# Four row tiles of A loaded ahead of B's second k-tile, a shorter warm-up, and an earlier bias in a matmul, bias and tanh kernel

## The chip, the cores and the metric

The kernel runs on one core of a Trainium2 chip. The metric is the device time of the whole program in microseconds (us). The profile's span covers the same execution without its first and last steps, and is some 2 us shorter. Engines: TensorE (PE), VectorE (DVE), ScalarE (ACT), GpSimd (POOL), which here issues nearly all loads, and SyncE (SP).

## The reference

```
a: 4096 x 4096, b: 4096 x 4096, bias: 4096, all float32
out = tanh(a @ b + bias)
```

## The kernel before

A and B are loaded as float32, cast to float16 on the way, and multiplied as 8192 matmuls of 128 x 128 by 128 x 512. The change concerns the first 100 us, where the rows of A come in two groups of four 128-row tiles and only a part of K is there yet. "Part one" uses eight k-tiles. Group 0's row tiles are transposed on PE itself (with an identity), into a PSUM bank, copied out half by DVE and half by ACT; group 1's are transposed by DVE.

```python
    WARM = 16
    ...
    for i in range(WARM):                       # warm-up matmuls on zeros
        nc.tensor.matmul(warm, zeros[:, :P], zeros, start=i == 0, stop=i == WARM - 1)
    load_b_low(nc.sync, raw_b, 0, 0, 1)         # B's first k-tile, as float32
    nc.scalar.copy(b_cur[0][:, 0, :], raw_b[:, 0, :])
    ...
    def turn_nat(m):
        tp = psum.tile([P, KS, P], fp16, name="tp", tag="ps")
        for t in range(KS):
            nc.tensor.transpose(tp[:, t, :], nat[m][:, :, t], ident)
        h = KS // 2
        nc.vector.tensor_copy(ats[m][:, ds(0, h), :], tp[:, ds(0, h), :])
        nc.scalar.copy(ats[m][:, ds(h, h), :], tp[:, ds(h, h), :])
    ...
    load_nat(0)
    load_nat(1)
    ...
    load_b_next()
    for m in (2, 3):
        load_nat(m)
        load_b_next()
    while b_done[0] < KS:
        load_b_next()
    want_a("g1a", 2, 4 * P, 2 * Q, 0, KS)       # group 1's first A
    ...
    turn_nat(0)
    turn_nat(1)
    row(0, 0, 1)
    row(1, 0, 1)
    across(ps, (0, 1), 1, 1, 0)
    turn_nat(2)
    row(2, 0, 2)
    across(ps, (0, 1, 2), 2, 1, 0)
    turn_nat(3)
    row(3, 0, 3)
    across(ps, range(G), 3, KS - 2 - 3, 0)
    ...
    for m in range(G):
        turn1(m, ("g1a", "g1b"), 0, KS)         # DVE transposes for group 1
    down(ps, KS - 2, KS, put_aside)
    group1(0, KS, put_aside, before1)
```

`row(m, t0, nt)` multiplies one row tile by k-tiles t0 and following (two matmuls each), `across` goes over several row tiles per k-tile, `down` ends one PSUM bank after another.

Of the kernel before, what the change touches and what calls it, by code (L numbers as in the profile page):

```python
# [23 lines left out]
def kernel(  # L24
# [7 lines left out]
    nc = tc.nc  # L32
# [8 lines left out]
    J = NCW // NB  # L41
    TB = 4
    G = 4
    KS = 8
    AN = 3
    KM = 16
    WARM = 16

    singles = ctx.enter_context(tc.tile_pool(name="singles", bufs=1))
    bpool = ctx.enter_context(tc.tile_pool(name="bpool", bufs=2))  # L50
# [14 lines left out]
    def load_b_low(queue, dst, n0, t0, nt):  # L65

        src = b[ds(0, P * KS), ds(n0, NCW)].rearrange("(x t) n -> x t n", t=KS)
        queue.dma_start(out=dst, in_=src[:, ds(t0, nt), :])  # L68
# [32 lines left out]
    def load_bias(bias_bc, n0, queue):  # L101
        src = bias[ds(n0, NCW)]
        queue.dma_start(
            out=bias_bc,
            in_=bass.AP(tensor=src.tensor, offset=src.offset, ap=[[0, P], *src.ap]),
        )
# [12 lines left out]
    def want_a(key, uses, *where):  # L119
        queue.append((key, uses, lambda: load_a(*where)))  # L120

    def want(load):
        queue.append((None, 0, load))

    def turn(at, key, mb0, t0, nt):
        pump()
        transpose_a(at, staged[key][0], mb0, t0, nt)
        staged[key][1] -= 1
        if not staged[key][1]:
            live[0] -= 1  # L130
            pump()

    def mm(ps, at, bt, t, j, start, stop):
        nc.tensor.matmul(  # L134
            ps, at[:, t, :], bt[t // TB][:, t % TB, ts(j, NB)], start=start, stop=stop
        )
# [27 lines left out]
    def aside(m, j):  # L164
        return spill[(m * J + j) // 4][:, (m * J + j) % 4, :]
# [9 lines left out]
    def add_bias(m, j):  # L175
        nc.vector.tensor_tensor(  # L176
            out=aside(m, j), in0=aside(m, j), in1=bias_bc[:, ts(j, NB)], op=mybir.AluOpType.add
        )
# [4 lines left out]
    def banks():  # L183
        return [[psum.tile([P, NB], fp32, name="ps") for j in range(J)] for m in range(G)]

    def load_b_all(t0, nt):
        for q in (0, 2, 1, 3):
            load_b(b_cur, 0, t0, nt, q)

    def across(ps, ms, t0, nt, first):  # L190
        for t in range(t0, t0 + nt):
            for m in ms:
                for j in range(J):
                    mm(ps[m][j], ats[m], b_cur, t, j, t == first, False)
# [22 lines left out]
    warm = psum.tile([P, NB], fp32, name="ps")  # L217
    for i in range(WARM):
        nc.tensor.matmul(warm, zeros[:, :P], zeros, start=i == 0, stop=i == WARM - 1)  # L219

# [9 lines left out]
    def load_nat(m):  # L230
        nc.gpsimd.dma_start(  # L231
            out=nat[m], in_=a[ds(m * P, P), ds(0, P * KS)].rearrange("m (x t) -> m x t", t=KS)
        )

    def load_b_next():
        t = b_done[0]
        b_done[0] += 1
        load_b_low(nc.gpsimd, b_cur[t // TB][:, ds(t % TB, 1), :], 0, t, 1)
# [8 lines that stand above are left out]
# [5 lines left out]
        out=ident, in_=ident, compare_op=mybir.AluOpType.is_equal, fill=0.0,  # L252
        base=0, pattern=[[-1, P]], channel_multiplier=1,
    )
    load_b_next()
    for m in (2, 3):
        load_nat(m)
        load_b_next()
    while b_done[0] < KS:
        load_b_next()  # L260
    want_a("g1a", 2, 4 * P, 2 * Q, 0, KS)
# [4 lines left out]
    want_a("g1c", 2, 4 * P, 2 * Q, KS, KM - KS)  # L266
    want_a("g1d", 2, 6 * P, 2 * Q, KS, KM - KS)
    bias_bc = biasp.tile([P, NCW], fp32, name="bias_bc")
    SA = [(KM, 8), (KM + 8, 8)]
    for t, nt in SA:  # L270
        want_a(("g0", t), G, 0, G * Q, t, nt)
        for u in range(t, t + nt, TB):
            want(lambda u=u: load_b_all(u, TB))
    want(lambda: load_bias(bias_bc, 0, nc.gpsimd))
    for m in range(G):
        want_a(("g1", m), 1, (G + m) * P, Q, KM, KT - KM)
    todo = [(c, mi) for c in range(NC) for mi in range(MT) if (c, mi) >= (0, 2 * G)]
# [1 line left out]
    ps = []  # L279

    def row(m, t0, nt):
        if len(ps) == m:
            ps.append([psum.tile([P, NB], fp32, name="ps") for j in range(J)])
        across(ps, (m,), t0, nt, 0)

    turn_nat(0)
    turn_nat(1)
    row(0, 0, 1)
    row(1, 0, 1)
    across(ps, (0, 1), 1, 1, 0)  # L290
    turn_nat(2)
    row(2, 0, 2)
    across(ps, (0, 1, 2), 2, 1, 0)
    turn_nat(3)
    row(3, 0, 3)
    across(ps, range(G), 3, KS - 2 - 3, 0)

    def turn1(m, keys, t, nt):
        turn(ats[G + m], keys[m // 2], (m % 2) * Q, t, nt)
# [1 line left out]
    def turn0(m, t, nt):  # L301
        turn(ats[m], ("g0", t), m * Q, t, nt)
# [14 lines left out]
    ps = banks()  # L317
# [5 lines left out]
    def before2(m, j):  # L323
        if m >= 2 * G - 2:
            turn0(2 * (m - 6) + j, *SA[0])

# [3 lines left out]
    ps = banks()  # L330
    for i, (t, nt) in enumerate(SA):
        for m in range(G):
            if i:
                turn0(m, t, nt)
        across(ps, range(G), t, min(t + nt, KT - TB) - t, KM)

    def turn2(m):
        turn(ats[G + m], ("g1", m), 0, KM, KT - KM)

    for m in range(2 * G):  # L340
        for j in range(J):
            add_bias(m, j)
    turn2(0)
    down(ps, KT - TB, KT, end)

# [26 lines left out]
    for i, (c, mi) in enumerate(todo):  # L372
        if mi == 0:
            b_cur, bias_bc = b_next, bias_next
# [21 lines left out]
        for j in range(J):  # L396
# [3 lines left out]
            for h in range(halves):  # L400
                ps = psum.tile([P, w], fp32, name="ps")
# [41 lines left out]
```

## Time and profile before

| | |
|---|---|
| time, median of 3 runs | 1785.43 us (1785.35 to 1785.65) |
| span of the profiled run | 1783.5 us |
| PE busy | 1776.8 us |
| first matmul of group 1 | 25.25 us |
| from there to the span's end | 1758.27 us, no wait of PE but at the very end |

One more excerpt of the timeline is needed, PE in the first 11 us (start, length, what, and in brackets the idle time before it with what ended it):

```profile
6.62 0.65 PE L243 MATMUL tp<-ident,nat 128*128 128x128 f16 x8
7.53 0.71 PE L243 MATMUL tp<-ident,nat 128*128 128x128 f16 x8 [0.26 <-DMA nat<-in_a_dram]
8.07 2.15 PE L134 MATMUL ps<-b,at 128*128 128x512 f16 x8
...
10.35 0.71 PE L243 MATMUL tp<-ident,nat 128*128 128x128 f16 x8
```

The second batch of transposes waited for the second row tile, which landed at 7.48 us.

### The profile page before, as it was taken

What the parts mean: (1) busy time and instruction counts of PE and PEld (TensorE: products, weight loads), DVE (VectorE), ACT (ScalarE), POOL (GpSimd) and SP (SyncE); (2) the same over time, 40 slices, a digit from 0 to 9 for tenths busy, and PEclk for the clock granted to TensorE, in tenths of its full rate; (3) what the DMA queues carried; (4) which work ended last, traced back from release to release, by engine and by line L of the source; (5) the groups of instructions that cost most, each with busy time, mean ns of one, the idle gap of its engine ahead of it and who ended that gap; (6) DMA issues with size and microseconds to landing.
All of it is one profiled execution on the core that took longest, in us unless ns stands there. A gap on an engine that the chain in (4) does not pass through costs nothing.

```text
span 1783.5 us, 20275 instructions
## 1 busy us (share of the span) xinstructions
PE 1776.8 (100%) x8272; PEld 808.7 (45%) x8272; DVE 856.6 (48%) x561; ACT 174.9 (10%) x281; POOL 607.3 (34%) x1126
## 2 busy tenths in 40 slices
PE   9999999999999999999999999999999999999999
PEld 4444444444444444444444444444444444444444
DVE  3774544455444544454444544454445544454442
ACT  3020000000000000000000000000000000000001
POOL 5454433232443333223343333223322233223310
PEclk9999999999999999999999999999999999999999
DMA  9999987676988866666698876666767666766731
GB/s 194 189 211 222 172 151 129 111 136 110 191 155 154 149 107 119 116 119 118 111 201 154 158 135 118 113 121 107 130 111 125 107 111 118 118 114 108 119 75 42
DMA packets 207916, 238.61 MB, mean 134 GB/s; under 512 B 22096, under 2 KB 157776, under 8 KB 207824
## 3 DMA queue, kind: packets, MB, share of 16 engines
q0 software_dynamic: 170384, 169.68, 65.2%
q1 hardware_dynamic: 37152, 67.52, 10.4%
q8 instruction: 64, 1.05, 0.2%
q14 instruction: 28, 0.23, 0.0%
q10 hardware_dynamic: 288, 0.13, 0.0%
HBM read 337.64 MB, written 67.11 MB: 227 GB/s over the span
## 4 chain that ended last, share of the span: by engine, by line
PE 99%; DMA 0%; issue 0%; POOL 0%; ACT 0%; DVE 0%; POOLq 0%; DVEq 0%
PE ps L404 93%; PE ps L134 6%; DMA nat<-in_a_dram 0%; POOL nat L231 0%; PE tp L243 0%; ACT o_sb L148 0%; DVE at L245 0%; DVE o_sb L145 0%; ACT at L246 0%; POOL b L68 0%; POOL ident L251 0%; POOLq L251 0%; DVEq L145 0%; POOLq L427 0%
## 5 line engine op out<-in xcount | busy, mean ns | idle before, releaser
L404 PE MATMUL ps<-b,at 128*128 128x512 f16 x7712 | 1657.8, 378 | 0.0
L404 PEld LDWEIGHTS <-at 128*128 128x128 f16 x7712 | 754.6, 98 | 903.3
L85 POOL DMA_DIRECT2D an<-in_a_dram x1004 | 542.4, 549 | 1059.4 <-DVE at L96 921.8
L96 DVE STREAM_TRANSPOSE at<-an 128x1024 f16<-128x1024 f16 x252 | 647.7, 2612 | 0.1
L145 DVE TENSOR_TENSOR o_sb<-ps,bias_bc 128x512 f32<-128x512 f32 (+1 forms) x243 | 166.2, 685 | 873.6 <-PE ps L404 752.4
L148 ACT ACTIVATE o_sb<-o_sb 128x512 f32<-128x512 f32 (+1 forms) x243 | 151.7, 625 | 1500.9 <-DVE o_sb L145 1500.9
L134 PE MATMUL ps<-b,at 128*128 128x512 f16 x256 | 56.4, 379 | 1.4 <-DVE at L245 1.0
L72 POOL DMA_DIRECT2D b<-in_b_dram x96 | 52.2, 548 | 14.3 <-DMA an<-in_a_dram 10.3
L134 PE MATMUL ps<-b,atx 128*128 128x512 f16 x256 | 55.8, 379 | 0.0
L134 PEld LDWEIGHTS <-at 128*128 128x128 f16 x256 | 24.8, 98 | 31.5 <-DVE at L245 1.9
L134 PEld LDWEIGHTS <-atx 128*128 128x128 f16 x256 | 24.9, 98 | 30.3 <-DVE atx L96 0.3
L96 DVE STREAM_TRANSPOSE atx<-an 128x1024 f16<-128x1024 f16 (+1 forms) x12 | 21.9, 1897 | 16.6 <-DMA an<-in_a_dram 16.6
L148 ACT ACTIVATE spill<-spill 128x512 f32<-128x512 f32 x16 | 9.9, 630 | 78.5 <-DVE spill L145 78.5
L68 POOL DMA_DIRECT2D b<-in_b_dram x13 | 8.3, 643 | 24.7 <-PE ps L404 22.6
L145 DVE TENSOR_TENSOR spill<-ps,spill 128x512 f32<-128x512 f32 x16 | 10.3, 675 | 9.0 <-PE ps L134 9.0
L176 DVE TENSOR_TENSOR spill<-spill,bias_bc 128x512 f32<-128x512 f32 x16 | 9.7, 683 | 7.3 <-DMA bias_bc<-in_bias_dram 7.3
L171 DVE TENSOR_TENSOR spill<-ps,spill 128x512 f32<-128x512 f32 x16 | 10.2, 676 | 4.3 <-PE ps L134 4.3
L168 ACT COPY spill<-ps 128x512 f32<-128x512 f32 x16 | 8.7, 605 | 15.7 <-PE ps L134 15.7
L245 DVE COPY at<-tp 128x512 f16<-128x512 f16 x4 | 1.7, 425 | 11.8 <-PE tp L243 11.8
L219 PE MATMUL ps<-zeros 128*128 128x512 f16 x16 | 5.5, 522 | 1.3 <-DVE zeros L215 1.3
L219 PEld LDWEIGHTS <-zeros 128*128 128x128 f16 x16 | 2.0, 128 | 4.3 <-issue 2.5
L243 PE MATMUL tp<-ident,nat 128*128 128x128 f16 x32 | 2.7, 228 | 0.4 <-DMA nat<-in_a_dram 0.3
(13 smaller groups left out, 12.9 us busy)
## 6 DMA issues: line engine op xcount, KB each, us to landing
an<-in_a_dram POOLq DMA_DIRECT2D x480, 192.0 KB, 6.5
out_dram<-o_sb SPq DMA_DIRECT2D x239, 256.0 KB, 3.4
an<-in_a_dram POOLq DMA_DIRECT2D x480, 64.0 KB, 2.5
b<-in_b_dram POOLq DMA_DIRECT2D x103, 256.0 KB, 8.5
b<-in_b_dram POOLq DMA_DIRECT2D x6, 1024.0 KB, 13.6
an<-in_a_dram POOLq DMA_DIRECT2D x32, 128.0 KB, 6.5
out_dram<-spill SPq DMA_DIRECT2D x16, 256.0 KB, 5.7
an<-in_a_dram POOLq DMA_DIRECT2D x12, 256.0 KB, 7.2
```

Source lines behind the costliest of these rows:

```text
L68: queue.dma_start(out=dst, in_=src[:, ds(t0, nt), :])
L72: nc.gpsimd.dma_start(out=bt[t0 // TB][ds(q * QP, QP), ds(t0 % TB, nt), :], in_=src.rearrange("(t p) n -> p t n", p=QP),)
L85: nc.gpsimd.dma_start(out=an[ds(q * QP, QP), :, ds((t - t0) * QP, n * QP)], in_=src.rearrange("(mb p) k -> p mb k", p=QP),)
L96: nc.vector.transpose(at[:, ds(t, n), :].rearrange("P t (mb p) -> P mb t p", p=QP), an[:, ds(mb0, Q), ds((t - t0) * QP, n * QP)].rearrange ...
L134: nc.tensor.matmul(ps, at[:, t, :], bt[t // TB][:, t % TB, ts(j, NB)], start=start, stop=stop)
L145: nc.vector.tensor_tensor(out=o_sb[:, piece], in0=ps[:, piece], in1=addend[:, piece], op=mybir.AluOpType.add)
L148: nc.scalar.activation(o_sb[:, piece], o_sb[:, piece], mybir.ActivationFunctionType.Tanh)
L168: nc.scalar.copy(aside(m, j), ps)
L171: nc.vector.tensor_tensor(out=aside(m, j), in0=ps, in1=aside(m, j), op=mybir.AluOpType.add)
L176: nc.vector.tensor_tensor(out=aside(m, j), in0=aside(m, j), in1=bias_bc[:, ts(j, NB)], op=mybir.AluOpType.add)
L219: nc.tensor.matmul(warm, zeros[:, :P], zeros, start=i == 0, stop=i == WARM - 1)
L404: nc.tensor.matmul(ps, at[:, t, :], b_cur[t // TB][:, t % TB, ds(c0, w)], start=t == 0, stop=t == KT - 1,)
```

## The change

Its intent: get the four row tiles in early, so that PE needs no B beyond the first k-tile until all four rows are running; don't make the first tile wait for the warm-up; and take DVE's wait for bias out of part three.

```diff
-    WARM = 16
+    WARM = 12
@@ loads
-    load_b_next()
-    for m in (2, 3):
-        load_nat(m)
-        load_b_next()
+    load_nat(2)
+    load_nat(3)
     while b_done[0] < KS:
         load_b_next()
@@ bias, ahead of the third k-stage's loads in place of behind them
+    want(lambda: load_bias(bias_bc, 0, nc.gpsimd))
     SA = [(KM, 8), (KM + 8, 8)]
 ...
-    want(lambda: load_bias(bias_bc, 0, nc.gpsimd))
@@ order on PE (the whole block shown in the kernel before)
-    turn_nat(0)
-    ...
-    across(ps, range(G), 3, KS - 2 - 3, 0)
+    for m in range(G):
+        turn_nat(m)
+        row(m, 0, 1)
+    across(ps, range(G), 1, KS - 2 - 1, 0)
@@ bias adds, in part three
+        for m in range(i * G, i * G + G):
+            for j in range(J):
+                add_bias(m, j)
 ...
-    for m in range(2 * G):
-        for j in range(J):
-            add_bias(m, j)
```

More of the change, by code (lines that the diff above doesn't have):

```diff
@@ L284, in row @@
         across(ps, (m,), t0, nt, 0)
-    turn_nat(0)
-    turn_nat(1)
-    row(0, 0, 1)
-    row(1, 0, 1)
-    across(ps, (0, 1), 1, 1, 0)
-    turn_nat(2)
-    row(2, 0, 2)
-    across(ps, (0, 1, 2), 2, 1, 0)
-    turn_nat(3)
-    row(3, 0, 3)
-    across(ps, range(G), 3, KS - 2 - 3, 0)
+    for m in range(G):
+        turn_nat(m)
+        row(m, 0, 1)
+    across(ps, range(G), 1, KS - 2 - 1, 0)
     def turn1(m, keys, t, nt):
```

## The prediction

> **What bounds the kernel now.** I first read the page. TensorE (PE) is busy 1776.8 of 1783.5 us and the clock row grants full speed in all forty slices, so only time in which PE starts late or waits can be saved. The chain of work that ended last says where that could be:
>
> ```profile
> 3.44 6.87 DMA nat<-in_a_dram
> 10.30 0.05 issue
> 10.35 0.73 PE tp L243 x8
> ...
> 11.10 0.44 DVE at L245
> ...
> 11.58 2.33 PE ps L134 x10
> 13.91 0.51 PE tp L243 x8
> ...
> 15.54 106.58 PE ps L134 x493
> 122.12 1654.20 PE ps L404 x7680
> ```
>
> The columns are start, length and what ran. From 15.54 us to 1776.3 us the chain is nothing but matmuls. Before that it hangs on the load of the third row tile of A, which lands at 10.30 us. The view of PE's waits over the whole run agrees that all waits belong to the start:
>
> ```profile
> PE ps L219 <- DVE zeros L215: 1.3, 1, 1.3
> PE ps L134 <- DVE at L245: 1.0, 2, 0.5
> PE tp L243 <- DMA nat<-in_a_dram: 0.3, 1, 0.3
> PE ps L134 <- ACT at L246: 0.2, 1, 0.2
> ```
>
> (Total, times, longest.) So I read the first 30 us of the timeline next:
>
> ```profile
> 1.26 5.52 PE L219 MATMUL ps<-zeros 128*128 128x512 f16 x16 [1.26 <-DVE zeros L215]
> ...
> 15.54 9.87 PE L134 MATMUL ps<-b,at 128*128 128x512 f16 x45 [0.22 <-ACT at L246]
> ...
> 23.00 7.98 DVE L96 STREAM_TRANSPOSE atx<-an 128x1024 f16<-128x1024 f16 x4 [8.13 <-DMA an<-in_a_dram]
> ...
> 25.25 13.50 PEld L134 LDWEIGHTS <-atx 128*128 128x128 f16 x64 [0.33 <-DVE atx L96]
> ```
>
> The last two lines decide the case. Group 0's 64 matmuls of part one end at 25.25 us (15.54 + 45 x 0.2157). Group 1 follows at 25.25 us, and its first weight load was held for 0.33 us by VectorE (DVE), not by PE: DVE's first transpose began when group 1's A landed, at 23.00 us, and ran until about 25.20 us (the tile's view gives 2.196 us for the longest of these). So two chains arrive together: PE's own work, and the loads of A for group 1. In windows of 1 us the DMA engines are fully busy from 3 us on (shares of 0.97 to 1.46), with about 200 GB/s written. The loads before them are therefore limited by bytes, not by their order.
>
> **What the Trainium skill says.** "TensorE: Matmul & The Clock Gate", Part 1, gives 426.7 ns between 512-column matmuls on a cold array and 215.7 ns on a warm one. The trace agrees: warm-up weight loads are 0.43 us apart up to 5.08 us, and 8128 matmuls from 25.25 to 1776.32 us average 0.2154 us. The same part says the warm-up is a budget of time (about 3.4 us), not a number of matmuls. Here the slow stretch lasts from 1.26 to about 5.1 us, so it agrees roughly. Part 4 of that page says transposes on PE don't count as busy for the clock in the same way; no run so far tests that. "DMA: Bandwidth & Descriptors", section "Issuing engines are not separate DMA queues", says all DMAs share the same 16 engines. The full DMA row above fits that. "VectorE: DVE Perf Modes", the errata section, gives (N+151)/0.96 ns for a float32 add, 691 ns for N = 512; the bias adds measure 683 ns.
>
> **The change part by part.**
>
> *Shorter warm-up.* The sixteenth warm-up matmul starts at 6.40 us. The ten slow ones stay; four fast ones go: 4 x 0.216 = 0.86 us, so warm-up would end near 5.76 us. The first row tile lands at 1.32 + 4.6 = 5.92 us (issue start plus the shortest landing of that tile's view). Its transposes then start near 5.97 us in place of 6.62 us: 0.65 us earlier.
>
> *Row tiles first.* Landings come about 1.25 us apart: 7.50 us for the second tile, then (from when GpSimd, waiting on old loads, goes on) near 8.75, 10.30, 11.5 and 12.8 us. These slots now hold tile 3, tile 4 and B's k-tiles 2 and 3. The third tile comes about 1.5 us earlier and the fourth about 2.5 us earlier. The last of these eleven loads lands when it did.
>
> PE's new order per row tile is eight transposes, a wait for DVE's copy, two matmuls. From before's rows: transposes until the copy starts 0.72 us (mean of 0.69, 0.74, 0.75 and 0.70), copy until the matmul 0.48 us (11.10 to 11.58), two matmuls 0.43 us; together 1.63 us. Starts of the tiles: 5.97, 7.60, 9.23, 10.86 us, each after its landing. The fourth row's first matmul starts at 10.86 + 1.20 = 12.06 us. Its second needs the PSUM bank that held the fourth tile's transposes (the built program still shows a ScalarE wait there), which costs 0.61 us before (14.93 to 15.54): 12.67 us. From there 64 - 7 = 57 matmuls remain: 57 x 0.2157 = 12.29 us, ending at 24.96 us. B's k-tile 2 is wanted about 12.9 us and is there at 11.5. So PE's side alone gains 25.25 - 24.96 = 0.29 us. Most of what is won at the front is lost to four separate transpose-copy-matmul round trips, where before other rows' matmuls filled some of that time.
>
> *What group 1 then waits for.* Eleven loads of the same size stand ahead of group 1's A, still with at most eight in flight, so it should land at 22.97 us again; DVE's transpose ends at 25.20 us and the weight load can go at 25.25 us. **The 0.29 us becomes a wait for DVE.** Net gain: 0.0 us, within the 0.1 to 0.2 us by which I guess a landing could shift.
>
> *Bias.* The load moves from 68.62 us to about 42 us in GpSimd's order, ahead of the third k-stage of group 0's A. It pushes the loads behind it back by its own DMA time. I estimate 2 to 2.5 us of engine time: in before, the following issues show extra waits of 2.17 and 1.48 us around it. Slack of what follows, from the landings that GpSimd waits for and when PE wants the data: group 0's A lands about 51.8 us and is transposed at 60.67; B's k-tiles 24 to 27 land by about 74.8 and are wanted at 80.5. The later A load is the tightest: it lands near 67.1 us, perhaps 69.5 now. But DVE would do eight bias adds first, 67.6 to 72.5 us (8 x 0.607 us, from 9.72 us for 16). Then come four transposes of together 4.60 us, done at 77.1 us; PE wants the first at 80.5 us (66.70 + 64 x 0.2157). All hold.
>
> The second lot of adds ends near 82 us in place of 89.24 us. Before, only this was close:
>
> ```profile
> 79.52 9.72 DVE L176 TENSOR_TENSOR spill<-spill,bias_bc 128x512 f32<-128x512 f32 x16 [7.32 <-DMA bias_bc<-in_bias_dram]
> ...
> 89.16 2.30 DVE L96 STREAM_TRANSPOSE atx<-an 128x2048 f16<-128x2048 f16 x1
> ...
> 94.12 27.51 PEld L134 LDWEIGHTS <-atx 128*128 128x128 f16 x128
> ```
>
> DVE waited 7.32 us for bias, and group 1's next transposes ended at 91.46 us, 2.7 us before PE wanted them. The change widens that slack to nearly 10 us, yet PE never waited there. Worth in time: 0.0 us.
>
> Sum: 0.0 us from the start, 0.0 us from the bias; 1785.43 stays, and I say 1785.4 us.
>
> **The rivals.**
> 1. *PE's gain comes through* (1784.8 to 1785.2 us). That needs group 1's A to land 0.2 to 0.3 us earlier. For it: DMA shares differ from 1 us to the next. Against it: the same bytes stand ahead in the same queue. If PE's wait were not held by DVE at all, it would still be 0.29 us at most.
> 2. *PE turns slower than worked out.* Each round trip that takes 0.1 us longer costs 0.4 us in sum, of which 0.29 us is covered: 1785.5 to 1785.7 us.
> 3. *The clock falls back.* Between 6 and 12.7 us PE now does real matmuls for only 0.43 of every 1.63 us, and the skill says transposes may not count. In before, matmuls after a gap from about 10.04 to 11.58 us without any ran at full rate (ten in 2.15 us), which speaks against it. If it happened, up to 3.4 us would run at half speed: some 8 to 16 matmuls at 0.216 us extra, minus the slack, 1787 to 1788.5 us. I give it one in twelve.
> 4. *The earlier bias load makes a new wait in part three.* Several us of slack stand against it, and it would cost 1 us at most.
>
> **Range and chances.** The three runs before lie within 0.30 us. Rivals 1 and 2 lie about 0.5 us either side, the clock is a thin upper tail. I predict 1785.4 us, 8 in 10 between 1784.9 and 1785.9 us. Two per cent is 35.7 us, more than the whole time until 25.25 us holds to lose, and a gain of that size isn't there: same 0.99, faster 0.003, slower 0.007.
>
> **What would show it.** Right: the first transposes start at about 6.0 us; the fourth row's second matmul at 12.7 us; the last matmul of group 0's part one ends near 25.0 us, and group 1's first weight load still starts at 25.25 us, now with PE itself waiting up to 0.3 us for DVE's transpose; DVE's first transpose still starts at 23.0 us; bias adds run as eight at 67.5 us and eight at 77 us; no PE wait after 26 us. Wrong: group 1's A landing clearly before 22.7 us (faster), PE's first 64 matmuls ending after 25.3 us, matmuls 0.43 us apart after 9 us, or a wait near 80 us (slower).

## The result, and the profile after

| | before | changed |
|---|---|---|
| time, median of 4 runs each | 1785.39 us (1785.31 to 1785.65) | 1785.92 us (1785.66 to 1786.05) |
| span of the profiled run | 1783.5 us | 1784.1 us |
| group 1's first matmul | 25.25 us | 25.82 us |

The ratio is 1.0003 (95% interval 0.9985 to 1.002). A ratio here is the mean time of one kernel's runs over that of the other's of the same rounds, so not quite the ratio of the medians. The median lies 0.02 us above the predicted range.

The books close: from group 1's first matmul to the span's end it is 1758.27 us before and 1758.26 us changed. From group 1 on the two kernels are equal; all of the 0.57 us of the profiled runs is lost before it. The chain of work of the changed kernel:

```profile
1.99 6.42 DMA nat<-in_a_dram
8.41 0.05 issue
8.46 0.72 PE tp L243 x8
...
9.68 0.61 PE ps L134 x2
10.28 0.50 PE tp L243 x8
...
11.29 0.61 PE ps L134 x2
11.90 0.50 PE tp L243 x8
...
13.52 109.16 PE ps L134 x505
```

It no longer hangs on the third row tile but on the *second*, issued at 1.99 us and landed at 8.41 us. From there on each tile takes its round of about 1.6 us, as worked out, and the unbroken stretch of matmuls begins at 13.52 us, where 12.67 us had been predicted. The timeline of PE around the first tile:

```profile
1.26 5.30 PE L219 MATMUL ps<-zeros 128*128 128x512 f16 x12 [1.26 <-DVE zeros L215]
6.36 0.79 PE L243 MATMUL tp<-ident,nat 128*128 128x128 f16 x8
7.67 0.60 PE L134 MATMUL ps<-b,at 128*128 128x512 f16 x2 [0.52 <-DVE at L245]
8.46 0.70 PE L243 MATMUL tp<-ident,nat 128*128 128x128 f16 x8 [0.18 <-DMA nat<-in_a_dram]
```

The twelve warm-up matmuls took nearly as long as sixteen had (5.30 against 5.52 us): none of them ran at full clock. The trace's clock record first shows the full clock at 6.67 us here, at 5.12 us in the kernel before; until then the warm-up's weight loads are 0.43 us apart. And the two lines at the end of part one:

```profile
23.57 7.99 DVE L96 STREAM_TRANSPOSE atx<-an 128x1024 f16<-128x1024 f16 x4 [10.72 <-DMA an<-in_a_dram]
...
25.79 13.51 PEld L134 LDWEIGHTS <-atx 128*128 128x128 f16 x64 [0.31 <-DVE atx L96]
```

Group 1's A came 0.57 us later too (DVE starts at 23.57, before at 23.00 us), so both chains ended together once more, at 25.8 us. The bias did what was intended:

```profile
68.16 4.88 DVE L176 TENSOR_TENSOR spill<-spill,bias_bc 128x512 f32<-128x512 f32 x8
72.96 4.62 DVE L96 STREAM_TRANSPOSE at<-an 128x1024 f16<-128x1024 f16 x4
77.50 4.86 DVE L176 TENSOR_TENSOR spill<-spill,bias_bc 128x512 f32<-128x512 f32 x8
82.28 2.30 DVE L96 STREAM_TRANSPOSE atx<-an 128x2048 f16<-128x2048 f16 x1
```

No wait for bias, both lots where they were expected, group 1's transpose 6.9 us earlier than before (89.16 us); and nothing of it reaches the time.

### The profile page after: what moved, and what is told of

Same layout as the page of the kernel before. It is cut to its first block, busy times and chain, and to the rows that moved or that the text cites. A ratio compares the mean times of both kernels' runs of the same rounds, so it can differ in the third digit from the quotient of the medians.

```text
span 1784.1 us, 20267 instructions
## 1 busy us (share of the span) xinstructions
PE 1776.6 (100%) x8268; PEld 807.8 (45%) x8268; DVE 857.2 (48%) x561; ACT 175.2 (10%) x281; POOL 605.0 (34%) x1126
## 4 chain that ended last, share of the span: by engine, by line
PE 99%; DMA 0%; issue 0%; DVE 0%; ACT 0%; POOL 0%; DVEq 0%; POOLq 0%
PE ps L395 93%; PE ps L134 6%; DMA nat<-in_a_dram 0%; PE tp L243 0%; DVE at L245 0%; ACT o_sb L148 0%; POOL nat L231 0%; DVE o_sb L145 0%; ACT at L246 0%; DVEq L145 0%; POOLq L418 0%
```

## The experiments

They ran on three chips, one for each set of four. The kernel before ran beside each set: on these chips its medians were 1785.78, 1785.87 and 1785.57 us, and single runs went from 1784.95 to 1787.48 us, far wider than the three runs that the prediction had. Much of that scatter isn't in the kernel: the time less the span was 1.69 to 3.25 us. The spans are steadier, and since the span is the start of group 1 plus 1758.24 to 1758.27 us in all fourteen profiles (the two of the prediction's pair and the twelve below), each run's span tells when its group 1 began. So spans are compared below, as medians.

The expectations speak of a load's "first share": the trace records sixteen completions for each load, its shares, and it has landed with the last. These times, like the clock's, are from the trace's records.

### First set: which part of the change costs

**The changed kernel again** (no edit).

> The changed kernel once more, for a second profile. Theory O (order): with all four row tiles of A first in the queue the second one lands late whatever else happens; it lands after 8.2 us again (8.41 in the first profile, 7.48 in the kernel before), the first 64 matmuls end near 25.8 us, and the time is 1785.8 to 1786.0 us. Rival C (chance): the one packet of 1.44 us at 4.87 us in the first profile was an accident of that run; now the second tile lands near 7.5 us, the 64 matmuls end near 25.0 us and the median falls to 1785.4 us.

Measured: median 1785.98 us against 1785.78; spans 1783.7, 1784.0, 1784.2, 1784.3 and 1786.9 us, median 1784.2 against 1783.8 of the kernel before. The second tile landed at 8.73 us, later still, with other packets being slow; so the 8.41 us was not one accident (rival C, which expected 7.5 us, fails). But the run of the profile was a surprise, 1788.95 us, with this in windows cut at the clock's changes (busy times of each engine, then the granted clock, DMA share, GB/s):

```profile
5.02:8.43 3.41, 1.56 (x12) 0.78 (x10) 0.38 (x1) 0.47 (x1) 1.61 (x4) 1.00 0.98 156
8.43:15.26 6.83, 5.66 (x30) 3.32 (x30) 0.89 (x3) 1.76 (x3) 2.84 (x5) 0.50 1.12 204
15.26:26.00 10.74, 10.03 (x46) 4.52 (x47) 3.58 (x3) 0.74 (x2) 7.12 (x12) 1.00 1.34 198
```

The *first* tile landed late (7.25 us), the warm-up had ended, PE was busy for only 1.56 us out of 3.41, and the clock went back to half for 6.83 us. The pair of matmuls that takes 0.60 us took 1.03 us. Group 1 began at 28.66 us.

**Only the order** (loads and PE order; 16 warm-up matmuls, old bias).

> Only the order: four row tiles first and one row at a time on the matmul engine; 16 warm-up matmuls and the old bias. Theory O: second tile lands at 8.2 us or later, the whole 0.5 us is here, 1785.8 to 1786.0 us. Rival C: 1785.4 us. Rival W (the shorter warm-up makes the slow clock last longer, 6.67 us against 5.12 us in the two profiles): 1785.4 us here, and the clock up near 5.1 us.

Measured: median 1786.69 us, spans 1783.9 to 1784.8, median 1784.5 us. The slowest of this set. Its second tile landed at 7.95 us, yet its transposes began at 8.91 us, because here the warm-up held the chain:

```profile
1.26 6.20 PE L219 MATMUL ps<-zeros 128*128 128x512 f16 x16 [1.26 <-DVE zeros L215]
7.30 0.65 PE L243 MATMUL tp<-ident,nat 128*128 128x128 f16 x8
```

The clock came up at 6.50 us, so sixteen matmuls lasted until 7.3 us, and group 1 began at 26.24 us. The rival that blamed the shorter warm-up for the loss falls: with sixteen matmuls the loss is no smaller. Between the changed kernel and this one the median spans differ by 0.3 us (1784.2 against 1784.5), but the runs overlap (1783.7 to 1786.9 against 1783.9 to 1784.8), so a gain by the shorter warm-up isn't shown. Theory O's 8.2 us for the second tile wasn't met either.

**Only the bias.**

> Only the bias: loaded in part two, added in two lots of eight. Theory O: nothing, 1785.4 us, and no wait of the matmul engine after 26 us. Rival B (the earlier bias load delays a later load by enough to matter): 1785.9 us, with a wait of the matmul engine between 40 and 95 us.

Measured: 1785.82 us, spans 1783.4 to 1784.0, median 1783.7 us against 1783.8. Nothing. In this profile of the *old* order the second tile landed at 8.01 us and the chain of work hung on it, not on the third (group 1 at 25.49 us).

**Only the warm-up of 12.**

```diff
-    WARM = 16
+    WARM = 12
```

> Only the warm-up of 12. Theory O: nothing, 1785.4 us, since the third row tile's landing at 10.3 us holds the chain in this order anyway. Rival W: the clock comes up later than 6 us in this profile too and the time is 1785.9 us.

Measured: 1785.85 us, spans 1783.6 to 1784.1, median 1784.0 us, within 0.2 us of the kernel before; the clock came up at 6.82 us and cost nothing that can be told from chance: these are rival W's numbers, but the kernel before had 1785.78 us beside it. The expectation's reason was wrong, though. The chain of work of this kernel, old order:

```profile
2.00 6.34 DMA nat<-in_a_dram
8.34 0.04 issue
8.39 0.73 PE tp L243 x8
...
16.13 106.57 PE ps L134 x493
```

The second tile landed at 8.34 us and group 1 began at 25.84 us. The old order loses to a late second tile as well: 7.53 gave 25.25, 8.05 gave 25.49, 8.39 gave 25.84 us. The profile of the kernel before had caught the earliest second tile of all.

### Second set: why the second tile is late, and whether the chain is the cause

**Other columns** (wrong result: third and fourth tile read elsewhere).

```diff
-  in_=a[ds(m * P, P), ds(0, P * KS)]...
+  in_=a[ds(m * P, P), ds(m // 2 * 2048, P * KS)]...
```

> The changed kernel, but the third and fourth row tiles are read from columns 2048 to 3071 of A (wrong result on purpose). In three profiles with the new order the DMA engines' first share of the eleventh load came at 18.40 to 18.52 us, in three with the old order at 18.06 to 18.19 us. Theory H (the four tiles slow each other because they are read at the same place of their rows): 18.0 to 18.2 us here. Rival F (four loads of A in succession are slow wherever they read): 18.4 to 18.5 us again. Time 1785.7 to 1786.3 us either way.

Measured: first share of the eleventh load at 18.15 us, which lies in H's range; but the second tile landed at 8.65 us, as late as ever, and spans were 1783.2 to 1784.3 us. The share doesn't decide it either: with the changed kernel's own loads it later came at 18.19 us (one tile for all rows) to 18.46 us (a warm-up of 8).

**B's second k-tile put back ahead of the third row tile.**

```diff
+    load_b_next()
     load_nat(2)
     load_nat(3)
```

> The changed kernel with B's second k-tile put back ahead of the third row tile. If four loads of A in succession make the queue slow, the eleventh load's first share comes at 18.1 to 18.2 us and the second row tile lands near 8.0 us. The matmul chain then hangs on the fourth row tile, which lands near 11.6 us instead of 10.9 us: third tile's transposes near 10.4 us, fourth's near 12.0 us, group 1's first matmul at 26.0 to 26.2 us, time 0.2 to 0.5 us over the changed kernel's. If succession doesn't matter: 18.4 us and the same lateness.

Measured: 1787.33 us against 1785.87, spans 1784.8, 1784.9, 1785.8 and 1786.8 us. The two longer runs show a mean clock of 0.999 and 0.998, the others 1.0, so the two undisturbed ones put the cost at about 1 us. The chain of work hangs on the third tile, where the fourth was expected:

```profile
3.45 7.40 DMA nat<-in_a_dram
10.85 0.05 issue
10.89 0.72 PE tp L243 x8
...
14.35 109.16 PE ps L134 x505
```

Group 1 began at 26.65 us. In the wait for the third tile PE was busy for 1.80 us of 3.41 (first busy time below), and the clock stayed full all the same (1.00, third number from the end):

```profile
10.23:13.64 3.41, 1.80 (x18) 1.34 (x18) 0.81 (x2) 0.59 (x1) 1.38 (x4) 1.00 1.11 207
```

For the queue's question it is a miss: the first share of the eleventh load came at 18.65 us, the latest of all, and the second tile at 8.31 us. So loads of A in succession don't explain the lateness; neither H nor F holds.

**Transposes one tile ahead.**

```diff
-    for m in range(G):
-        turn_nat(m)
-        row(m, 0, 1)
-    across(ps, range(G), 1, KS - 2 - 1, 0)
+    turn_nat(0)
+    for m in range(1, G):
+        turn_nat(m)
+        row(m - 1, 0, 1)
+    across(ps, range(G - 1), 1, 1, 0)
+    row(G - 1, 0, 2)
+    across(ps, range(G), 2, KS - 2 - 2, 0)
```

> The changed kernel with each row tile transposed before the row of the tile ahead of it is multiplied, and B's second k-tile used before the fourth row. Theory P (the chain of four transposes, copies and row matmuls, hung up on the second row tile's landing, sets when group 1 starts): the chain now has slack of about 1 us, the matmul engine is ready near 24.7 us and group 1 starts when its own A is transposed, 24.8 to 25.7 us; the span is 1783.1 to 1783.9 us, some 0.4 us under the changed kernel's and 0.1 to 0.3 us under that of the kernel before. Rival (group 1's load sets it in both): spans as the changed kernel's, 1783.8 to 1784.3 us.

Measured: 1785.36 us against 1785.87, spans 1783.3 to 1783.7, median 1783.4 against 1783.8 us. With PE's chain slack, the chain of work turns to group 1's load:

```profile
14.70 8.16 DMA an<-in_a_dram
...
22.98 2.08 DVE atx L96
25.06 0.05 issue
25.11 96.87 PE ps L134 x448
```

The second tile was late here too (8.15 us) and no longer mattered. Theory P holds, and its rival (group 1's load sets the start in both) fails.

**A warm-up of 8.**

```diff
-    WARM = 12
+    WARM = 8
```

> The changed kernel with 8 warm-up matmuls: they end near 4.7 us, so the matmul engine is idle for at least 0.9 us before the first row tile. One run in nine of the changed kernel took 3 us more, with the clock at half from 8.43 to 15.26 us after an idle stretch. Theory K (the clock follows how busy the matmul engine is in a window, so the shorter warm-up and the sparse row order put it at risk): now most runs are at 1788 us or more, with half the clock until 10 us or later. Rival (the slow run was an accident that has nothing to do with the warm-up): 1785.5 to 1786.3 us as with 12.

Measured: 1789.17 us; spans 1783.3, 1785.6, 1787.2, 1787.6 and 1787.9 us. In the profile the clock was up from 4.42 us, and down again from 7.84 to 18.08 us:

```profile
1.26 3.44 PE L219 MATMUL ps<-zeros 128*128 128x512 f16 x8 [1.26 <-DVE zeros L215]
5.59 0.71 PE L243 MATMUL tp<-ident,nat 128*128 128x128 f16 x8 [0.89 <-DMA nat<-in_a_dram]
6.82 0.60 PE L134 MATMUL ps<-b,at 128*128 128x512 f16 x2 [0.52 <-DVE at L245]
8.27 1.07 PE L243 MATMUL tp<-ident,nat 128*128 128x128 f16 x8 [0.84 <-DMA nat<-in_a_dram]
9.86 1.03 PE L134 MATMUL ps<-b,at 128*128 128x512 f16 x2 [0.52 <-DVE at L245]
```

This fits theory K: with eight, four runs of five are 1.8 us or more behind the kernel before. Two of them show a mean clock of 0.997, the profiled one among them. The other two (1785.6 and 1787.9 us) show 1.0, which doesn't count the time before the clock first comes up; how they lost theirs is not shown. The fifth, at 1783.3 us, shows that it stays a matter of timing.

### Third set: the prediction's own number, and a better version

**The changed kernel a third time.**

> The changed kernel a third time, beside the versions below on one chip. By the chain: second tile lands between 7.9 and 8.8 us (it did in nine of ten profiles), group 1 starts 17.2 to 17.4 us after the second tile's transposes do, so at 25.4 to 26.1 us; spans 1783.7 to 1784.4 us, with the chance of one run 3 us longer with the clock at half.

Measured: 1785.71 us against 1785.57; spans 1783.6 to 1783.8, median 1783.8 against 1783.6 us. The second tile landed at 8.01 us, but its transposes began only at 8.26 us, because here the first tile held the chain. It landed at 6.43 us, later than the warm-up needed (6.36 us in the first profile), and its first weight load waited for it:

```profile
6.47 0.68 PEld L243 LDWEIGHTS <-nat 128*128 128x128 f16 x8 [0.81 <-DMA nat<-in_a_dram]
```

The clock came up at 6.85 us, amid these transposes. Group 1 began at 25.57 us.

**One tile for all four rows** (wrong result).

```diff
-            nc.tensor.transpose(tp[:, t, :], nat[m][:, :, t], ident)
+            nc.tensor.transpose(tp[:, t, :], nat[0][:, :, t], ident)
```

> The changed kernel, but all four rows transpose the first row tile (wrong result on purpose), so no transpose after the first waits for a load; all loads stay. If the prediction failed only in the landing it assumed, the four tiles now start 1.6 us apart, the matmul engine is ready for group 1 about 19 us after the first tile's transposes start (24.9 to 25.5 us), and group 1's own A, 24.7 to 25.8 us, often comes later: spans 1783.0 to 1783.9 us, under those of the changed kernel. If the round trips themselves cost more than worked out, spans stay at 1783.8 to 1784.3 us.

Measured: spans 1783.2 to 1783.7, median 1783.45 us against 1783.8 of the changed kernel in the same set. The timeline:

```profile
6.03 0.65 PE L243 MATMUL tp<-ident,nat 128*128 128x128 f16 x8
7.64 0.66 PE L243 MATMUL tp<-ident,nat 128*128 128x128 f16 x8
9.26 0.66 PE L243 MATMUL tp<-ident,nat 128*128 128x128 f16 x8
10.88 0.65 PE L243 MATMUL tp<-ident,nat 128*128 128x128 f16 x8
...
25.04 0.98 PEld L134 LDWEIGHTS <-atx 128*128 128x128 f16 x6 [0.41 <-DVE atx L96]
```

This is the prediction's own picture: tiles at 6.03, 7.64, 9.26 and 10.88 us (predicted 5.97, 7.60, 9.23 and 10.86; the first tile's landing at 5.91 us was by chance where it had been predicted), after which group 1 waits for DVE's transpose. Its loads are those of the changed kernel, and the second tile landed late (8.11 us) as ever; only nothing waited for it.

**Group 1's first A also ahead of B's eighth k-tile** (on top of the transposes ahead).

```diff
-    while b_done[0] < KS:
+    while b_done[0] < KS - 1:
         load_b_next()
     want_a("g1a", 2, 4 * P, 2 * Q, 0, KS)
+    want(load_b_next)
...
-    across(ps, range(G), 2, KS - 2 - 2, 0)
+    across(ps, range(G), 2, KS - 1 - 2, 0)
...
-    down(ps, KS - 2, KS, put_aside)
+    down(ps, KS - 1, KS, put_aside)
```

> The version with transposes ahead, with group 1's first A load also put ahead of B's eighth k-tile, and that k-tile used last. Group 1's A lands near 21.5 us, its transpose is done near 23.9 us, and the start of group 1 falls to the matmul chain, 24.7 to 25.0 us: spans 1783.0 to 1783.3 us, 0.2 to 0.4 us under the version with transposes ahead alone (1783.4 us). If B's eighth k-tile now comes too late (after 23.0 us), as much is lost again: 1783.4 to 1783.8 us.

Measured: 1785.41 us, spans 1782.8 to 1783.9, median 1783.4 us; the same as without it, so a miss. In this profile group 1's A came at about 22.9 us rather than 21.5, and PE waited 0.39 us for B's eighth k-tile (landed at 23.42 us), the loss foreseen as the second case.

**The same with 16 warm-up matmuls.**

```diff
-    WARM = 12
+    WARM = 16
```

> The same with 16 warm-up matmuls. The second tile lands at 8 us or later, so a warm-up that ends at 6.6 to 7.5 us with a first transpose after it costs nothing: same spans as with 12, within 0.2 us, and no run with the clock at half. If the first tile's transposes end after the second tile is there (warm-up to 7.5 us, transposes to 8.2 us), at most 0.2 us more.

Measured: 1784.90 us against 1785.57 us (ratio 0.9996, interval 0.9983 to 1.0008: by time alone no difference is resolved), spans 1782.5 to 1783.4, median 1782.9 us against 1783.6 of the kernel before and 1783.8 of the changed one. It is better than with 12, by more than was expected. PE:

```profile
7.67 0.72 PE L243 MATMUL tp<-ident,nat 128*128 128x128 f16 x8 [0.22 <-DMA nat<-in_a_dram]
...
11.06 13.38 PE L134 MATMUL ps<-b,at 128*128 128x512 f16 x60
24.28 1.89 PE L134 MATMUL ps<-b,atx 128*128 128x512 f16 x8
```

Its second tile landed at 7.63 us, early by luck, so part of its lead over the version with 12 is chance; the two can't be told apart by five runs each. Correct in result, it is the version to keep: its median span is the lowest, 0.7 us (0.04%) under the kernel before.

### What these runs say together

| kernel | warm-up | clock up at | 2nd tile lands | its transposes start | group 1 starts |
|---|---|---|---|---|---|
| before | 16 | 5.12 | 7.48 | 7.53 | 25.25 |
| only bias | 16 | 4.92 | 8.01 | 8.05 | 25.49 |
| only warm-up | 12 | 6.82 | 8.34 | 8.39 | 25.84 |
| only order | 16 | 6.50 | 7.95 | 8.91 | 26.24 |
| changed | 12 | 6.67 | 8.41 | 8.46 | 25.82 |
| changed, third time | 12 | 6.85 | 8.01 | 8.26 | 25.57 |
| other columns | 12 | 5.93 | 8.65 | 8.69 | 26.07 |
| transposes ahead | 12 | 6.01 | 8.15 | 8.20 | 25.11 |

All in us. In the new order (only order, changed, other columns) group 1 starts 17.3 to 17.4 us after the second tile's transposes do; in the old order 17.4 to 17.7 us, by the late ones 17.45. So for a second tile at the usual 8.0 to 8.7 us the two orders are worth nearly the same. Nor is it shown that the new order makes the second tile late: it landed at 7.48 to 8.34 us in the three profiles with the old order of loads, at 7.95 to 8.73 us in the seven with the changed kernel's loads.

## Why the prediction was wrong

**What bounds the kernel: right.** PE's matmuls from group 1 on never wait, in either kernel, and the start of group 1 is the whole of the difference.

**The bias: right.** It predicted 0.0 us, eight adds near 67.5 and eight near 77 us, and no PE wait; the profile has 68.16 and 77.50 us and no wait, and the bias alone measures 1783.7 against 1783.8 us.

**The round trips: right.** 1.63 us each was predicted; 1.61 us was measured where no tile waits for a load (one tile for all rows). The second PSUM bank's wait (predicted 0.61 us) was 13.52 - 12.91 = 0.61 us.

**The step that failed: the landings** ("7.50 us for the second tile ... Starts of the tiles: 5.97, 7.60, 9.23, 10.86 us, each after its landing"). The starts were 6.36, 8.46, 10.12 and 11.73 us. The second tile landed at 8.41 us, not 7.50; the 0.86 us that its transposes slipped is the whole difference between the predicted end of PE's chain, 24.96 us, and the measured 25.82 us. The number came from one profile and was used as if it were a property of the kernel. In fourteen profiles the second tile landed between 7.48 and 8.73 us (the first between 5.52 and 7.25 us), and 7.48 us, the profile that the prediction was read from, was the earliest: bad luck in the draw, but one draw was all that the step rested on. The old order has its late ones too (8.01, 8.34 us), and in those profiles its chain hung on the second tile as well. That PE's chain, hung on a row tile's landing, is the cause is shown by three runs: without the wait for it the tiles start as predicted (one tile for all rows), with slack for it the chain leaves PE (transposes ahead), and where the third tile was made late the chain hung on that (B put back). Why the second tile lands when it does was tested twice and not found; it stays open.

**A second term of the same kind: the end of the warm-up** ("The ten slow ones stay; four fast ones go ... warm-up would end near 5.76 us"). It held only if the clock comes up at 5.1 us. In fourteen profiles it came up between 4.42 and 6.85 us. In the changed kernel's first profile all twelve were slow and the transposes began at 6.36 us. There the second tile's landing hid it. In the profile with only the order changed, it was the warm-up that set the chain.

**A third: "it should land at 22.97 us again".** DVE began on group 1's A at 23.57 us, not 23.00, and its transpose let group 1 go at 25.79 us. So in the changed kernel's first profile either lateness alone would have cost over 0.5 us; PE's chain was the last by 0.03 us. In the other profiles of the new order it was the last by more (25.57 against 25.44 us in the third one). Nor is it shown that the new order's queue runs behind: group 1's A landed at 22.22 to 23.45 us in the seven profiles with the changed kernel's loads, at 22.38 to 22.88 us in the three with the old ones, and the same bytes lie ahead of it. What does go with a late landing is when a packet of the instruction queue falls (last section), but that was seen and not tested, so it stays open.

**Readings that were a little off.** The DMA shares from 3 us on reach 1.49 (19 to 20 us), not 1.46. And 22.97 us is near DVE's start; by the trace group 1's A had landed at 22.88 us. Neither moves the sum.

**The range.** Its width came from three runs that lay within 0.30 us. The kernel before itself later ran from 1784.95 to 1787.48 us in 27 runs. The changed kernel's later medians, 1785.98 and 1785.71 us, are 0.20 and 0.14 us over those of the kernel before beside them, the first one 0.53 us. A loss of some 0.1 to 0.5 us is what these say, at the limit of what they can tell. That the first median fell 0.02 us outside the range and the third 0.19 us inside it is chance; the wrong landing is not.

**The rivals.** Rival 3, the clock falling back, was given one in twelve and 1787 to 1788.5 us. It happened in one of fourteen runs, at 1788.95 us. It played no part in the median. Its doubt whether transposes on PE count for the clock, for which the prediction names the skill, can now be answered for these runs: take windows of 3.41 us from when the clock came up. With the transposes, the two windows that lost the clock had the least PE time of all (1.56 and 1.60 us, against 1.80 us or more in those that kept it). Without them they had more (0.84 and 0.89 us) than two that kept it (0.61 us with B put back, 0.76 us with group 1's A earlier). So here the transposes look like counting. Rival 1 did not come; rival 2 had the right sign but the wrong cause, since the rounds took 1.67 and 1.61 us.

## What to carry to other kernels

A landing time read from one profile is a draw, not a constant: before an order of work is hung on it, look at several profiles, and ask what the order costs at the late end. The order that won here didn't need an early tile: it put each tile's transposes a step ahead of the matmuls that use them, so that the second tile's lateness no longer set group 1's start (25.11 us with a landing at 8.15 us); what set it then was group 1's own load. And a shorter warm-up is a risk while real work is still sparse: in this order four matmuls less made no difference clear of the scatter, eight less put the median 3.3 us behind the kernel before.

## What the Trainium skill lacked or had wrong

- "TensorE: Matmul & The Clock Gate", Part 1, says that the clock's transition varies by ±500 ns from run to run, since its window is free-running. Here it came up between 4.42 and 6.85 us in fourteen profiles, a spread of 2.4 us, with PE's first matmul always at 1.26 us. (The page also speaks of 6, 11 or 14 slow matmuls for one kernel, which fits better: (4.42 - 1.26)/0.43 to (6.85 - 1.26)/0.43 is 7 to 13.)
- The same page advises no idle gaps of PE over about 3 us, and ties the fall of the clock to an idle window. Here it fell with no single gap over 1.5 us: after a window of 3.41 us in which PE was busy for 1.56 us (gap 1.43 us) and, with a warm-up of 8, after one with 1.60 us (gaps 0.89, 0.52 and 0.84 us at most). Other windows kept it, the sparsest of them with 1.80 us (B's second k-tile put back). By these few cases the line runs between 47% (1.60 us) and 53% (1.80 us) busy, as this profile counts busy. At half clock, a window with 2.79 us did not bring it back, one with 2.87 us did. The time at half clock was 6.83 and 10.24 us, which agrees with two and three windows of the page's 3413 ns.
- "DMA: Bandwidth & Descriptors" has no figure for the scatter of a landing. Loads of 256 KB (as written) behind an identical queue landed 7.48 to 8.73 us (second load) after the start, and single packets of 2,048 bytes that usually take 0.173 us took up to 1.50 us between 4.8 and 7.3 us.
- "Runtime: NRT & Kernel Launch" calls the cost of fetching the next 16 KiB of instructions mostly hidden; no page gives the time that it takes from the DMA engines. In every trace one packet of 16,384 bytes of the instruction queue, 0.89 to 0.98 us long, falls between 19 and 26 us. In the changed kernel's first profile it started at 21.39 us, and fifteen of sixteen completions of group 1's fourth load were in by 22.45 us, the last one at 23.45 us. In the twelve profiles that load group 1's A behind all of B's first k-tiles, it landed at 22.57 to 23.45 us where the packet started by 21.39 us (seven profiles), at 22.22 to 22.72 us where it started at 21.51 us or later (five). This was seen, not tested.
